# A hybrid decoder layer on one core: the recurrence's second pair mirrored in the array, attention's values channel-major, the first inverse ranked ahead

## The chip, the cores and the metric

The kernel is one launch on one NeuronCore of a Trainium2 chip. The metric is device time in microseconds (us). Before the change three runs took 1244.15, 1249.96 and 1253.78 us; the median is 1249.96 us.

## The reference, cut to what matters

One decoder layer on a sequence of 512 tokens of width 1024, all in fp32. A combined projection of the normalized input gives three attention groups, the inputs of an RWKV-7 recurrence and two branch gates; both mixers are projected, gated and added to the residual; a gated MLP with a short convolution follows.

```python
h = rms_norm(x, norm1_w) * (1 + sc1) + sh1             # sc1, sh1.. = c @ w_ada + b_ada
att_in, rwkv_in, gate_in = split(h @ w_in)
y_att  = attention_mixer(att_in) @ w_att_out            # 3 (window, dilation) groups of 8 heads x 64
y_rwkv = rwkv7_mixer(rwkv_in, ...) @ w_rwkv_out         # 16 heads x 64
x = x + gt1 * ((sig(g_att) * y_att + sig(g_rwkv) * y_rwkv) @ w_o)
x = rms_norm(x + gt2 * conv_ffn(adaLN(x)))
# recurrence, per head; state is 64 x 64
sa = state @ aa_t
state = state * w_t + sa (x) bb_t + v_t (x) k_t ;  y_t = state @ r_t
# attention: out = sum over groups of share_g * softmax(q k^T) v ; share_g from the groups' denominators
```

## The kernel before, in words

**Products.** A matmul with 512 columns is done three times on fp32r halves (high x high, low x high, high x low), so that the names `hhi`, `hlo`, `whi`, `wlo` recur. The halves of weights are made by ScalarE (`whi`) and VectorE (`wlo`, L1139). Small products are plain fp32; the trace has two records for each of them, so "x8" of a small product is four matmuls.

**Order.** From the start to the gates everything is written as tasks with an engine, a cost in us, a priority and a due rank (`Plan`, `pl.add`). A simulated run over these costs fixes one order for each engine, and each engine then takes its instructions in that order. The 512-column products of projections (`body`) have the lowest priority on TensorE and stand where the plan expected a gap; tasks of the recurrence (`C_` = 0) go first. VectorE's work for pair m of the recurrence has rank `V_ + 0.1 m` = 200 + 0.1 m, and the inverse of group g the rank `I_ + (0.1, 0.2, 0.5, 0.6)[g]`, `I_` = 200.15.

**Attention.** Groups 1 and 2 are held in one permuted order, so there are two sets of results, `o[0]` and `o[1]`. `attend` takes one token block `n` and one pair of heads `i` at a time: scores (tile `sc`), exponentials, transposes (`pt`, copied to `pts`), and `values` (tile `po`, L831 ff): for each head a matmul with 128 tokens of `pts` as weights and 64 channels of `v` as columns, which gives tokens on partitions. At the end VectorE scales `o` by each head's share (L1017), TensorE turns 32 blocks of 128 x 128 into channels (tile `pa`, L151) and adds the two groups on the way, and four DMAs store `att_d`. Tasks with `open` in their name, and with them the loads for the recurrence's pairs (L1256), come after all of this.

**Recurrence.** 16 heads are 8 pairs m of two heads; a group g is two pairs (i = 0, 1), so there are 4 groups. `pair` makes a pair's operands: `ar` (a and r of 64 tokens side by side), `bk`, its transpose `bkt`, the masked products `gt` (grams: tile `pg<-ar,bk` on TensorE, masked by VectorE at L1397). `inverse` solves a triangular system per chunk on VectorE (tiles `lt`, `tt`, L1453 to L1519) and ends with two sets of 32 x 32 products on TensorE (tile `pe`). `chain` then goes through 8 chunks c of 64 tokens, both pairs together:

- `state`: `xy` = `mbd` (the state) times `ar` for both pairs, 128 x 128 x 128, then four 64 x 64 x 64 products of `gt` and `uv` added to the half X of `xy`. R and X are the partition halves of results and of the unknowns; they swap from chunk to chunk and are the same for both pairs;
- ScalarE copies the half X (`xs`, L1621); `solve`: four products 64 x 64 x 64 into `u`; ScalarE copies them into `uv` (L1658);
- `update`: four products with 128 rows and 64 weight columns into `w` (trace: `u<-uv,bkt`), where the two heads of a pair go to the two partition halves by turns; VectorE makes the next `mbd` (L1641);
- `outs`: four products with 128 rows and 64 weight columns that are added to the half R of `xy` (trace: `xy<-uv,gt 128*64`), copied by ScalarE (L1652);
- every second chunk `values`: two products 128 x 128 x 128 (`u<-cen,v`).

Groups g and g + 2 share a room of SBUF, so the projections of group 2 start after chain 0, those of group 3 after chain 1. `t<-ident,yt` turns a chain's results at its end.

Of the kernel before, what the change touches and what calls it, by code (L numbers as in the profile page):

```python
# [128 lines left out]
class Layer:  # L129
# [502 lines left out]

    def mask2(self):
# [38 lines left out]
    def attention(self):  # L672
# [4 lines left out]
        o = [ap.tile([P, 4, ATT_W], F32, name="o0"), None]  # L677
# [110 lines left out]
        def attend(gi, hf, order, blocks, width, mask, V, ready, prio):  # L788
# [4 lines left out]
            for n, i, new, end in order:  # L793
# [37 lines left out]
                def values(n=n, i=i, d=d, new=new, end=end):  # L831
                    if new:
                        pos[n] = self.aps.tile([P, 256], F32, tag="po", name=self.n("po"), bufs=2)
                    vs = V(n)
                    for h in range(2):
                        cs = slice(i * P + h * 64, i * P + h * 64 + 64)
                        for j, v in enumerate(vs):
                            self.mm(pos[n][:, cs], d["pts"][:, h, j * P : (j + 1) * P], v[:, cs],
                                    new and h == 0 and j == 0, end and h == 1 and j == len(vs) - 1)

                def out(n=n, i=i, new=new):
                    c0, c1 = (i * P if new else 0), i * P + P
                    if gi and o[1] is None:
                        o[1] = ap.tile([P, 4, ATT_W], F32, tag="o1", name="o1")
                    nc.scalar.copy(o[gi][:, n, hf * 256 + c0 : hf * 256 + c1], pos[n][:, c0:c1])
# [11 lines left out]
                t = pe(0.9 * wd / 256, values, [t], S0, take=("po",) if new else (), give=("pts",), name="po")  # L857
# [110 lines left out]
        for _ in ada:  # L968
            pass

# [23 lines left out]
        scaled = []  # L994
        for gi in range(2):
# [19 lines left out]
            def scale(n, gi=gi, ea=ea):  # L1015
                ov = o[gi][:, n, :].rearrange("p (h e) -> p h e", h=8)
                nc.vector.tensor_tensor(ov, ov, ea[:, n, :].unsqueeze(2).to_broadcast([P, 8, 64]), op=ALU.mult)  # L1017
            t = dve(0.6, diff, [got[gi], *stats[gi]], name="al")
            t = sca(0.45, exps, [t], name="al")
            t = dve(1.2, share, [t], name="al")  # L1020
            scaled += [dve(0.7, lambda n=n, scale=scale: scale(n), [t, *outs[gi]], name="al") for n in range(4)]
        for i in range(4):
            d = {}

            def turn(i=i, d=d):
                d["pa"] = self.aps.tile([P, S], F32, tag="pt", name=self.n("pa"), bufs=2)
# [196 lines left out]
    def pair(self, g, i):  # L1223
# [98 lines left out]
        def a_row():  # L1322
# [3 lines left out]
            nc.vector.scalar_tensor_tensor(halves(d["ar"], 1), c8(d["k"]), ch(self.kkn), pex(), op0=ALU.mult,  # L1326
                                           op1=ALU.mult)
# [5 lines left out]
        ar = dve(0.75, a_row, [k, ex, gr["room"]])  # L1333
# [6 lines left out]
        def norm():  # L1340

            pn = d["pn"] = self.psx("pn")
# [3 lines left out]
        def norms():  # L1346
            if i == 0:
                gr["sq"] = gp.tile([P, 16], F32, tag="sq", name=self.n("sq"), bufs=1)
            for x in range(2):
                nc.scalar.copy(gr["sq"][64 - 64 * x : 128 - 64 * x, 8 * i : 8 * i + 8], d["pn"][64 * x : 64 * x + 64, :8])  # L1350
# [33 lines left out]
        def gram(q):  # L1384
# [4 lines left out]
            for cc in range(4):  # L1389
                col = (cc % 2) * 2 + cc // 2  # L1390
# [38 lines left out]
    def inverse(self, g):  # L1429
# [6 lines left out]
        I = I_ + (0.1, 0.2, 0.5, 0.6)[g]  # L1436
# [128 lines left out]
    def chain(self, g):  # L1565
# [18 lines left out]
        def values(c):  # L1584
            for i in range(2):
                self.mm(d["u"][:, i * P : (i + 1) * P], prs[i]["v"][:, c * C : (c + 2) * C], self.cen, i == 0, i == 1)

        def value(c, x):
            uv = uvs[c + x] = cw.tile([P, 256], F32, tag="uv", name=self.n("uv"), bufs=3)
            nc.scalar.copy(uv[64 * x : 64 * x + 64, :], d["u"][64 * x : 64 * x + 64, :])  # L1590
# [5 lines left out]
        norms, all_ = [], []  # L1596

        def vals(c):
            t = pe(0.54, lambda: values(c), [start, last_uv])
            for x in range(2):  # L1600
                uvd[c + x] = sca(0.38, lambda x=x: value(c, x), [t], C_ + 0.01 * x, take=("uv",))
        vals(0)
        for c in range(NCH):
            e, q, cp = c % 2, c // 4, (c % 4) // 2
            r0, x0 = (0, 64) if e == 0 else (64, 0)
            R, X = slice(r0, r0 + 64), slice(x0, x0 + 64)
            gt = lambda i, h, rows, cols, e=e, q=q, cp=cp: prs[i]["gt"][rows, e, 4 * q + 2 * cp + h, cols]
            s = {}

            def state(c=c, q=q, s=s, gt=gt, R=R, X=X):  # L1610
                xy = s["xy"] = ps("xy", bufs=2)
# [526 lines left out]
```

## Time and profile before

| what | us |
|---|---|
| runs, median of 3 | 1249.96 |
| the profiled execution, own time | 1247.44 |
| its span, first to last instruction | 1245.7 |
| TensorE busy in the span | 1197.4 |
| VectorE busy | 746.5 |
| ScalarE busy | 545.4 |
| GpSimd busy | 118.2 |

The profiled execution's own time is the span and 1.74 us around it, and lies 2.52 us below the median of the runs. In the profile PE is TensorE's matmuls, PEld its weight loads, DVE VectorE, ACT ScalarE, POOL GpSimd. A row of a timeline gives its start, its length and how many records it merges; matmuls overlap, so what one takes of the engine is the distance from its start to the next row's start, less an idle time that the next row shows in brackets.

### The profile page before, as it was taken

To read this page: it belongs to the slowest core of one execution; us is meant where nothing else is said; L and a number is where in the kernel's file an instruction comes from. 1 tells how busy PE (TensorE), PEld (TensorE's weight loads), DVE (VectorE), ACT (ScalarE), POOL (GpSimd) and SP (SyncE) were. 2 spreads that over 40 slices of the span, in tenths; PEclk is the share of its full clock that TensorE was granted. 3 is DMA by queue.
4 is the path that set the end of the run, shared out by engine and by line. 5 is a ranking of instruction groups with operands and counts; after the bars stand their busy time and mean duration, and the time that the engine had idled before them with its cause. 6 is when DMAs were issued, how large, how long until landed. Compare 5 with 4: busy or idle time off the path is not lost.

```text
span 1245.7 us, 18047 instructions
## 1 busy us (share of the span) xinstructions
PE 1197.4 (96%) x7012; PEld 976.5 (78%) x7012; DVE 746.5 (60%) x1242; ACT 545.4 (44%) x981; POOL 118.2 (9%) x235
## 2 busy tenths in 40 slices
PE   4999999999999999999999799999999999999997
PEld 3788878888787877777787577788888888878886
DVE  6697862422678968536896844555556566552235
ACT  4484522523566373455445343334443434442133
POOL 4000000000001013030002222214100000000001
PEclk9899999999999999999999789999999999999999
DMA  9745871130333332322330424571133332323331
GB/s 316 242 143 163 274 235 49 46 85 1 92 99 88 97 89 77 110 60 82 92 105 26 146 79 132 174 219 34 56 97 96 90 102 85 102 87 116 102 119 68
DMA packets 168900, 139.39 MB, mean 112 GB/s; under 512 B 8849, under 2 KB 150251, under 8 KB 168815
## 3 DMA queue, kind: packets, MB, share of 16 engines
q1 hardware_dynamic: 168671, 137.98, 36.5%
q8 instruction: 55, 0.90, 0.3%
q14 instruction: 30, 0.25, 0.1%
q10 hardware_dynamic: 144, 0.26, 0.1%
HBM read 127.65 MB, written 10.56 MB: 111 GB/s over the span
## 4 chain that ended last, share of the span: by engine, by line
PE 82%; DVE 8%; DMA 5%; ACT 2%; issue 1%; SPq 0%; POOL 0%; POOLq 0%; DVEq 0%; ACTq 0%
PE u L148 23%; PE o L148 13%; PE v L148 7%; PE pg L148 7%; PE qk L148 6%; PE xy L148 4%; PE pr L148 3%; DMA araw<-in_w_ada_dram 3%; PE k L148 3%; PE pa L148 2%; PE r L148 2%; PE early L148 2%; PE po L148 2%; PE sc L148 1%; PE pt L151 1%
## 5 line engine op out<-in xcount | busy, mean ns | idle before, releaser
L194 DVE TENSOR_TENSOR wlo<-raw,whi 128x1024 fp32r<-128x1024 f32 x67 | 84.1, 1255 | 151.0 <-ACT whi L193 150.9
L148 PE MATMUL u<-h2lo,whi 128*128 128x512 f32 (+2 forms) x368 | 142.3, 387 | 0.0
L148 PE MATMUL u<-h2hi,whi 128*128 128x512 f32 (+2 forms) x368 | 142.3, 387 | 0.0
L148 PE MATMUL u<-h2hi,wlo 128*128 128x512 f32 (+2 forms) x368 | 142.2, 386 | 0.0
L1136 ACT CAST whi<-raw 128x1024 fp32r<-128x1024 f32 (+2 forms) x73 | 72.5, 993 | 130.2 <-PE qk L148 49.5
L193 ACT CAST whi<-raw 128x1024 fp32r<-128x1024 f32 x67 | 70.3, 1049 | 112.0 <-PE o L148 53.8
L1139 DVE TENSOR_TENSOR wlo<-raw,whi 128x1024 fp32r<-128x1024 f32 (+2 forms) x73 | 84.2, 1154 | 22.9 <-ACT whi L1136 22.7
L148 PEld LDWEIGHTS u<-h2hi,wlo 128*128 128x128 f32 x368 | 68.9, 187 | 15.7
L148 PEld LDWEIGHTS u<-h2lo,whi 128*128 128x128 f32 x368 | 68.9, 187 | 15.7 <-POOL h2lo L405 0.2
L148 PEld LDWEIGHTS u<-h2hi,whi 128*128 128x128 f32 x368 | 68.9, 187 | 15.5
L1983 DVE SCALAR_TENSOR_TENSOR u<-u,cols,u 128x511 f32<-128x511 f32 x88 | 65.6, 746 | 4.2 <-ACT u L1981 2.7
L148 PE MATMUL qk<-hhi,wlo 128*128 128x512 f32 x160 | 63.9, 400 | 0.0
L148 PE MATMUL qk<-hlo,whi 128*128 128x512 f32 x160 | 63.6, 397 | 0.0
L148 PE MATMUL qk<-hhi,whi 128*128 128x512 f32 x160 | 63.5, 397 | 0.0
L148 PE MATMUL o<-whi,fhi 128*128 128x512 f32 x144 | 56.1, 390 | 0.3 <-DVE u L1983 0.3
L148 PE MATMUL o<-wlo,fhi 128*128 128x512 f32 x144 | 56.0, 389 | 0.0
L148 PE MATMUL o<-whi,flo 128*128 128x512 f32 x144 | 56.0, 389 | 0.0
L148 PE MATMUL pg<-hhi,wlo 128*128 128x512 f32 x128 | 52.0, 406 | 0.0
L148 PE MATMUL pg<-hlo,whi 128*128 128x512 f32 x128 | 51.8, 405 | 0.0
L148 PE MATMUL pg<-hhi,whi 128*128 128x512 f32 x128 | 51.3, 401 | 0.0
L810 DVE CUSTOM_DVE_ANT_0 sm<-sc,m 128x256 f32<-128x256 f32 (+1 forms) x64 | 24.0, 405 | 37.6 <-PE sc L148 36.5
L347 DVE SCALAR_TENSOR_TENSOR acc<-araw,cols,acc 128x1024 f32<-128x1024 f32 x28 | 35.9, 1282 | 17.2 <-DMA araw<-in_w_ada_dram 17.1
(404 smaller groups left out, 2824.0 us busy)
## 6 DMA issues: line engine op xcount, KB each, us to landing
raw<-in_w_in_dram SPq DMA_DIRECT2D x62, 512.0 KB
raw<-in_w_up_dram SPq DMA_DIRECT2D x44, 512.0 KB
araw<-in_w_ada_dram SPq DMA_DIRECT2D x32, 512.0 KB
raw<-in_w_down_dram SPq DMA_DIRECT2D x22, 512.0 KB
araw<-in_w_ada_dram SPq DMA_DIRECT2D x32, 256.0 KB
wvraw<-in_w_in_dram SPq DMA_DIRECT2D x20, 256.0 KB
gate_d<-gs SPq DMA_DIRECT2D x16, 256.0 KB
gate<-gate_d SPq DMA_DIRECT2D x16, 256.0 KB
```

Of the source, the lines that this page charges most:

```text
L148: return self.nc.tensor.matmul(out, lhsT, rhs, start=start, stop=stop)
L151: self.nc.tensor.matmul(out, in_, self.ident[: in_.shape[0], : in_.shape[0]], is_transpose=True, start=start, stop=stop,)
L193: self.nc.scalar.copy(hl[0], raw)
L194: (lo_eng or self.nc.vector).tensor_tensor(hl[1], raw, hl[0], op=ALU.subtract)
L347: nc.vector.scalar_tensor_tensor(d["acc"], raw, ck, d["acc"], op0=ALU.mult, op1=ALU.add)
L810: nc.vector.tensor_tensor_reduce(d["sm", h][:, :wd], d["sc"][h][:, :wd], m[:, 256 - wd : 256] if gi == 0 else m[:, :wd], 1.0, 3.0e38, op0= ...
L1136: nc.scalar.copy(d["w"][0], d["raw"])
L1139: nc.vector.tensor_tensor(d["w"][1], d["raw"], d["w"][0], op=ALU.subtract)
L1983: nc.vector.scalar_tensor_tensor(u[:, d:], pu[:, : S - d], ch(c), u[:, d:], op0=ALU.mult, op1=ALU.add)
```

## The change

Four things are done.

1. **The second pair is mirrored.** For pair i = 1 the halves R and X are swapped, in `ar`, `bk`, `gt` (index `x ^= i`), in the norms, and in the chain. `xy` now holds only the unknowns' half of both pairs (128 columns, pair 0 in one partition half, pair 1 in the other), a new tile `xo` holds the results' halves, and the state's product is done in two tasks, `state` and `state_out`, each with two matmuls of 64 weight columns. The four products of `state`, `solve` and `outs` are written with the pair as inner loop (`ih`), so that the pairs take turns.
2. **Copies follow.** `xs` and `out` copy 128 x 128 in place of 64 x 256; `uv` is two chunks in one tile, and the solved values are copied by two copies in a row in place of one. At the end of a chain two turns of `yts` by x are each followed by two half-size `y` operations.
3. **Attention's values** have 64 channels of `v` as weights and 128 tokens of `pts` as columns, with the two heads on the two partition halves by turns, so `o` is channel-major. The share of each head is turned (8 small transposes), split into a high and a low part, spread over the channels by 8 products with 40 rows and 512 columns (tile `pw`), multiplied by VectorE and added by GpSimd in place of ScalarE's copy. GpSimd writes the constant rows for this (`share_rows`).
4. **The inverse of group 0** has the rank `I_ - 0.2` = 199.95 (before 200.25), ahead of all pairs' ranks.

```diff
-        I = I_ + (0.1, 0.2, 0.5, 0.6)[g]
+        I = I_ + (-0.2, 0.2, 0.5, 0.6)[g]
...
-            r0, x0 = (0, 64) if e == 0 else (64, 0)
-            R, X = slice(r0, r0 + 64), slice(x0, x0 + 64)
+            R = [slice(64 * (e ^ i), 64 * (e ^ i) + 64) for i in range(2)]
+            X = R[::-1]
...
-                if c:
-                    for i in range(2):
-                        self.mm(xy[:, i * P : (i + 1) * P], prs[i]["ar"][:, c, :], mbd(i), i == 0, False)
-                for j, (i, h, cs) in enumerate(hs):
-                    self.mm(xy[X, cs], gt(i, h, R, X), s["uv"][R, cs], c == 0 and j == 0, j == 3)
+                for i in range(2 if c else 0):
+                    self.mm(xy[X[i], :P], prs[i]["ar"][:, c, X[i]], mbd(i), True, False)
+                for i, h, cs, ci in ih:
+                    self.mm(xy[X[i], cs], gt(i, h, R[i], X[i]), s["uv"][R[i], ci], c == 0 and h == 0, h == 1)
+
+            def state_out(c=c, s=s, R=R):
+                s["xo"] = ps("xo")
+                for i in range(2 if c else 0):
+                    self.mm(s["xo"][R[i], :P], prs[i]["ar"][:, c, R[i]], mbd(i), True, False)
...
-                for j, (i, h, cs) in enumerate(hs):
-                    self.mm(d["u"][X, cs], gt(i, h, X, X), s["xs"][X, cs], j == 0, j == 3)
+                for i, h, cs, _ in ih:
+                    self.mm(d["u"][X[i], cs], gt(i, h, X[i], X[i]), s["xs"][X[i], cs], h == 0, h == 1)
...
-            for i in range(2):
-                self.mm(d["u"][:, i * P : (i + 1) * P], prs[i]["v"][:, c * C : (c + 2) * C], self.cen, i == 0, i == 1)
+            for n, i, x in ((0, 0, 0), (0, 1, 0), (1, 1, 1), (1, 0, 1)):
+                r = 64 * (i ^ x)
+                self.mm(d["u"][r : r + 64, n * P : n * P + P], prs[i]["v"][:, (c + x) * C : (c + x + 1) * C], self.cen,
+                        n == 0, n == 1)
...
-            last_uv = sca(0.38, lambda s=s, X=X: nc.scalar.copy(s["uv"][X, :], d["u"][X, :]), [so])
+            last_uv = sca(0.28, lambda solved=solved: solved(0), [so])
+            last_uv = sca(0.28, lambda solved=solved: solved(1), [last_uv])
...
-                            self.mm(pos[n][:, cs], d["pts"][:, h, j * P : (j + 1) * P], v[:, cs],
-                                    new and h == 0 and j == 0, end and h == 1 and j == len(vs) - 1)
+                            self.mm(pos[n][h * 64 : h * 64 + 64, i * P : i * P + P], v[:, c0 : c0 + 64],
+                                    d["pts"][:, h, j * P : (j + 1) * P], new and j == 0, end and j == len(vs) - 1)
...
-                for n in range(4):
-                    self.tr(d["pa"][:, n * P : (n + 1) * P], o[0][:, n, i * P : (i + 1) * P], n == 0, False)
-                for n in range(4):
-                    self.tr(d["pa"][:, n::4], o[1][:, n, i * P : (i + 1) * P], False, n == 3)
+                self.mm(d["w", gi], self.heads[:, i * P : (i + 1) * P], self.share[gi], True, True)
...
+                nc.gpsimd.tensor_tensor(d["t"], o[0][:, i, :], o[1][:, i, :].rearrange("p (r j) -> p j r", r=4), op=ALU.add)
```

How the instructions stand: TensorE in chain 0, one chunk from `state` to after `solve`, before (sizes in the order are those of the result, so `64x64 x4` are four matmuls):

```order
L148 MATMUL xy_4403<-mbd_86,ar_3240 128x128
L148 MATMUL xy_4403<-mbd_87,ar_3358 128x128
L148 MATMUL xy_4403<-uv_4384,gt_3299 64x64 x4
L148 MATMUL pg_4210<-hlo,whi_4018 128x512
L148 MATMUL pg_4210<-hhi,wlo_4019 128x512
L148 MATMUL pg_4210<-hhi,whi_4018 128x512
L148 MATMUL pg_4210<-hlo,whi_4018 128x512
L148 MATMUL u_4082<-xs_4412,gt_3299 64x64 x4
L148 MATMUL pg_4210<-hhi,wlo_4019 128x512
```

The same place in the changed kernel:

```order
L148 MATMUL xy_4391<-mbd_86,ar_3232 64x128
L148 MATMUL xy_4391<-mbd_87,ar_3325 64x128
L148 MATMUL xy_4391<-uv_4376,gt_3357 64x64 x4
L148 MATMUL xo_4402<-mbd_86,ar_3232 64x128
L148 MATMUL xo_4402<-mbd_87,ar_3325 64x128
L148 MATMUL pw_4407<-lw,l2h_3777 128x512
L148 MATMUL pa_4408<-la,l2h_3777 128x512
L148 MATMUL pw_4407<-lw,l2l 128x512
L148 MATMUL pa_4408<-la,l2l 128x512
L148 MATMUL u_4066<-xs_4405,gt_3357 64x64 x4
L148 MATMUL pg_4122<-hhi,whi_4042 128x512
```

Two matmuls of the state are now four, of half the weight columns each, and stand on both sides of the 64 x 64 products; as many filler products stand between `state` and `solve`.

TensorE in chain 0 at the end of an even pair of chunks, `update`, `values` and `outs`, before:

```order
L148 MATMUL u_4082<-uv_4250,bkt_3241 64x64 x2
L148 MATMUL u_4082<-uv_4250,bkt_3359 64x64 x2
L148 MATMUL u_4082<-cen,v_3213 128x128
L148 MATMUL u_4082<-cen,v_3457 128x128
L148 MATMUL xy_4342<-uv_4250,gt_3299 64x64 x4
L148 MATMUL pg_4210<-hhi,wlo_4019 128x512
```

and now:

```order
L148 MATMUL u_4066<-uv_4222,bkt_3233 64x64 x2
L148 MATMUL u_4066<-uv_4222,bkt_3326 64x64 x2
L148 MATMUL u_4066<-cen,v_3196 64x128
L148 MATMUL u_4066<-cen,v_3399 64x128 x2
L148 MATMUL u_4066<-cen,v_3196 64x128
L148 MATMUL xo_4329<-uv_4222,gt_3357 64x64 x4
L148 MATMUL pg_4122<-hhi,wlo_4043 128x512
```

The three tasks stay together, and all of their products now have 64 weight columns.

VectorE at the start of group 0's inverse (`lt`, `tt`, `sup` are its tiles; `wlo`, `v`, `kk`, `rl` and the masked `gt` belong to later pairs), before:

```order
L1371 SCALAR_TENSOR_TENSOR kk_719_3636<-k_3604,cols,na_3423 128x512
L1471 TENSOR_TENSOR lt_3620<-lt_3620,rn_3578 128x1024
L1139 TENSOR_TENSOR wlo_3644<-raw_3543,whi_3643 128x1024
L1149 SCALAR_TENSOR_TENSOR v_3670<-v_3582,mu_122,sh 128x512
L1475 MEMSET lt_3620 128x32
L1478 COPY sup_3679<-lt_3620 128x14
L1479 MEMSET lt_3620 128x14
L1380 TENSOR_TENSOR rl_3673<-kk_719_3636,rh_3672 128x512
L1505 TENSOR_TENSOR tt_3656<-tt_3656,lt_3620 128x4
```

and now:

```order
L1411 SCALAR_TENSOR_TENSOR kk_723_3626<-k_3609,cols,na_3450 128x512
L1506 STREAM_TRANSPOSE lt_3635<-ld_3600 128x32x32
L1511 TENSOR_TENSOR lt_3635<-lt_3635,rn_3581 128x1024
L1182 SCALAR_TENSOR_TENSOR v_3673<-v_3585,mu_122,sh 128x512
L1515 MEMSET lt_3635 128x32
L1518 COPY sup_3680<-lt_3635 128x14
L1519 MEMSET lt_3635 128x14
L1172 TENSOR_TENSOR wlo_3660<-raw_3512,whi_3659 128x1024
L1437 TENSOR_TENSOR gt_3662<-pg_733_3663,mask 128x2x2x128
L1437 TENSOR_TENSOR gt_3662<-pg_734_3664,mask 128x2x2x128
L1545 TENSOR_TENSOR tt_3675<-tt_3675,lt_3635 128x4
```

From group 0's last mask to the end of its inverse VectorE has 87 instructions before and 82 now. On TensorE 1219 products of 512 columns stand ahead of group 0's first `pe` product before, and 1227 now, 8 of which are the new `pw` products of attention. Ahead of group 1's they are 1389 and 1435, of group 2's 1782 and 1784, of group 3's 1872 and 1880; ahead of the last grams of group 3 1815, with chain 2 in its third chunk, and now 1812, with chain 2 in its second.

## Rows read from the trace of the kernel before

**Rows 1.** The page, part 1: TensorE; and busy time of each engine by stretches (us from the start; PE, PEld, DVE, ACT, POOL busy, in brackets the instructions; then the granted clock, 1.00 being 2.4 GHz and 0.50 1.2 GHz, DMA share and GB/s). The cuts 434, 508 and 707 are the ends of the inverses of groups 0, 1 and 3, 645 is that of group 2, and 668 is the last mask of group 3.

```profile
PE 1197.4 (96%) x7012; PEld 976.5 (78%) x7012; DVE 746.5 (60%) x1242; ACT 545.4 (44%) x981; POOL 118.2 (9%) x235
...
345.00:434.00 89.00, 88.74 (x468) 71.23 (x466) 77.62 (x133) 49.56 (x78) 4.95 (x10) 1.00 0.34 94
434.00:508.00 74.00, 73.76 (x647) 58.11 (x646) 56.99 (x114) 39.08 (x81) 17.00 (x30) 1.00 0.32 94
508.00:645.00 137.00, 135.77 (x972) 106.79 (x972) 89.64 (x156) 67.67 (x125) 17.37 (x34) 1.00 0.29 82
...
668.00:707.00 39.00, 33.03 (x265) 25.38 (x264) 30.88 (x72) 15.92 (x36) 12.11 (x21) 0.89 0.35 113
707.00:773.00 66.00, 62.07 (x542) 48.09 (x543) 30.98 (x59) 30.41 (x68) 15.34 (x27) 0.86 0.27 80
```

**Rows 2.** The same view in steps of 5 us around the start of chain 3.

```profile
695.00:700.00 5.00, 2.73 (x30) 2.23 (x29) 4.79 (x10) 1.42 (x3) 2.64 (x3) 0.82 0.65 210
...
710.00:715.00 5.00, 3.00 (x69) 2.63 (x69) 3.13 (x6) 3.21 (x6) 0.00 (x0) 0.50 0.22 58
715.00:720.00 5.00, 4.15 (x24) 3.34 (x24) 4.92 (x9) 3.45 (x8) 0.00 (x0) 0.50 0.79 217
720.00:725.00 5.00, 5.00 (x25) 3.70 (x25) 3.02 (x7) 2.39 (x5) 1.27 (x2) 0.50 0.44 140
725.00:730.00 5.00, 5.00 (x33) 3.75 (x31) 1.89 (x5) 2.85 (x8) 0.00 (x0) 0.95 0.18 56
```

**Rows 3.** TensorE's timeline in chain 0 (start, length, operation, records merged).

```profile
464.69 0.40 PE L148 MATMUL pg<-hhi,whi 128*128 128x512 f32 x1
465.01 0.68 PE L148 MATMUL u<-xs,gt 64*64 64x64 f32 x8
465.62 0.50 PE L148 MATMUL pg<-hlo,whi 128*128 128x512 f32 x1
465.95 0.40 PE L148 MATMUL pg<-hhi,wlo 128*128 128x512 f32 x1
...
466.75 0.45 PE L148 MATMUL u<-uv,bkt 128*64 128x64 f32 x8
467.13 0.71 PE L148 MATMUL u<-cen,v 128*128 128x128 f32 x4
467.77 0.68 PE L148 MATMUL xy<-uv,gt 128*64 128x64 f32 x8
468.38 0.50 PE L148 MATMUL pg<-hhi,wlo 128*128 128x512 f32 x1
...
469.41 0.40 PE L148 MATMUL pg<-hhi,whi 128*128 128x512 f32 x1
469.65 0.61 PE L148 MATMUL xy<-mbd,ar 128*128 128x128 f32 x4
470.19 0.68 PE L148 MATMUL xy<-uv,gt 64*64 64x64 f32 x8
470.79 0.50 PE L148 MATMUL pg<-hlo,whi 128*128 128x512 f32 x1
...
473.65 0.45 PE L148 MATMUL u<-uv,bkt 128*64 128x64 f32 x8
473.94 0.63 PE L148 MATMUL xy<-uv,gt 128*64 128x64 f32 x8
474.50 0.50 PE L148 MATMUL pg<-hhi,whi 128*128 128x512 f32 x1
```

**Rows 4.** TensorE's timeline at the end of group 2's inverse.

```profile
645.73 1.20 PE L148 MATMUL pe<-lt,gt 32*32 32x32 f32 x64
646.86 0.50 PE L148 MATMUL pg<-hlo,whi 128*128 128x512 f32 x1
```

**Rows 5.** TensorE's timeline in attention: one `values`.

```profile
237.61 0.39 PE L148 MATMUL qk<-hhi,wlo 128*128 128x512 f32 x1
237.84 1.00 PE L148 MATMUL po<-v,pts 128*128 128x64 f32 x8
238.65 0.48 PE L148 MATMUL qk<-hhi,whi 128*128 128x512 f32 x1
```

**Rows 6.** The chain of waits: the first products after the last transfer of w_ada, and the end of attention (start, length, what).

```profile
188.34 2.20 PE v L148 x8
...
329.07 1.66 PE pa L151 x13
...
331.36 5.76 DMA att_d<-attT
...
337.19 0.60 ACT attT L1034
...
340.04 1.90 DMA l<-in_a_dram
```

**Rows 7.** VectorE's timeline: group 3's last mask and the last operation of its inverse; and TensorE's waits for VectorE's inverses (total us, times, longest).

```profile
666.99 0.68 DVE L1397 TENSOR_TENSOR gt<-pg,mask 128x512 f32<-128x512 f32 x1
...
706.42 0.71 DVE L1519 STREAM_TRANSPOSE lt<-tt 128x512 f32<-128x512 f32 x1
...
PE pe L148 <- DVE lt L1519: 3.2, 2, 2.9
```

**Rows 8.** Groups of GpSimd's instructions: its additions of two 128 x 512 tiles (busy us, mean ns of one, idle before them).

```profile
L1875 POOL TENSOR_TENSOR gate<-gate,gate 128x512 f32<-128x512 f32 x8 | 11.2, 1403 | 45.0 <-DVE gate L1874 45.0
```

More of the change, by code (lines that the diff above doesn't have):

```diff
@@ L631, in masks, with share_rows @@
                 pattern=[[-1, P]], channel_multiplier=1)
+    def share_rows(self):
+        nc = self.nc
+        self.heads = self.awl.tile([P, 2, S], F32R, tag="qk12", name="heads", bufs=1)[:40, 0, :]
+        t = self.awl.tile([P, 2, S], F32R, tag="qk02", name="share", bufs=1)[:40]
+        self.share = [t[:, gi, :] for gi in range(2)]
+        one = lambda r, c: self.ident[r, c : c + 8].unsqueeze(2).to_broadcast([r.stop - r.start, 8, 64])
+        h = self.heads.rearrange("p (h e) -> p h e", e=64)
+        for r, c in ((slice(0, 32), 0), (slice(32, 40), 32)):
+            nc.gpsimd.tensor_copy(h[r], one(r, c))
+        for x in self.share:
+            nc.gpsimd.tensor_copy(x[:32].rearrange("p (h e) -> p h e", e=64), one(slice(0, 32), 64))
     def mask2(self):
@@ L1013, in share @@
                 nc.vector.tensor_tensor(ea, ea, dn, op=ALU.mult)
[L1015 to L1017 removed]
             t = dve(0.6, diff, [got[gi], *stats[gi]], name="al")
             t = sca(0.45, exps, [t], name="al")
[L1020 to L1021 removed]
+            shares.append((dve(1.2, share, [t], name="al"), ea))
@@ new lines, in attention, with turn, hi, lo @@
+        parts = []
+        for gi in range(2):
+            d = {}
+            def turn(gi=gi, d=d):
+                d["ps"] = self.aps.tile([P, S], F32, tag="pt", name=self.n("pe"), bufs=2)
+                for n in range(4):
+                    self.tr(d["ps"][:8, n * P : (n + 1) * P], shares[gi][1][:, n, :], n == 0, n == 3)
+            def hi(gi=gi, d=d):
+                nc.scalar.copy(self.share[gi][:8], d["ps"][:8])
+            def lo(gi=gi, d=d):
+                nc.vector.tensor_tensor(self.share[gi][32:40], d["ps"][:8], self.share[gi][:8], op=ALU.subtract)
+            t = pe(0.48, turn, [shares[gi][0], heads], take=("pt",), name="pa")
+            t = sca(0.6, hi, [t], name="pa")
+            parts.append(dve(0.7, lo, [t], give=("pt",), name="pa"))
@@ new lines, in out @@
+            def out(i=i, d=d):
+                d["t"] = self.awl.tile([P, S], F32, tag="attT", name=self.n("attT"), bufs=2)
+                nc.gpsimd.tensor_tensor(d["t"], o[0][:, i, :], o[1][:, i, :].rearrange("p (r j) -> p j r", r=4), op=ALU.add)
+            ts = []
+            for gi in range(2):
+                t = pe(0.24, lambda gi=gi, turn=turn: turn(gi), [parts[gi]], take=("pt",), name="pa")
+                ts.append(dve(0.7, lambda gi=gi, scale=scale: scale(gi), [t, *outs[gi]], give=("pt",), name="pa"))
@@ L1037, in attention @@
+            t = pl.add("POOL", 1.2, out, ts, E_, take=("attT",), name="pa")
             pl.add("DMA", 0.8, lambda i=i, d=d: nc.sync.dma_start(self.att_d[:, i, :], d["t"]), [t], W_, lag=2.0,
@@ L1595, in chain @@
         mb, uvd, last_uv = [], {}, start
-        norms, all_ = [], []
+        norms, all_, used = [], [], []
         def vals(c):
             t = pe(0.54, lambda: values(c), [start, last_uv])
-            for x in range(2):
-                uvd[c + x] = sca(0.38, lambda x=x: value(c, x), [t], C_ + 0.01 * x, take=("uv",))
+            t = sca(0.38, lambda: value(c, 0), [t], C_, take=("uv",))
+            uvd[c] = uvd[c + 1] = sca(0.38, lambda: value(c, 1), [t], C_)
         vals(0)
@@ L1665, in chain @@
                 vals(c + 1)
-            ou = pe(0.47, outs, [last_uv], C_ + 0.02, name="xr")
-            yt = sca(0.38, out, [ou], C_ + 0.05, take=("yts",) if c == 0 else (), give=("xy",))
-            pl.join([ou] + ([up] if c < NCH - 1 else []), give=("uv",))
+            ou = pe(0.35, outs, [last_uv, so_], C_ + 0.02, name="xr")
+            yt = sca(0.29, out, [ou], C_ + 0.05, take=("yts",) if c == 0 else (), give=("xo",))
+            used.extend([ou] + ([up] if c < NCH - 1 else []))
+            if e:
+                pl.join(used, give=("uv",))
+                used = []
             d["yt", c] = yt
@@ L1675, in chain @@
         g2, gg, ys = {}, {}, {}
-        fin = []
+        fin, after = [], []
         for i in range(2):
```

125 lines of the change are left out of this document (72 added, 53 removed).

## The prediction

> **What bounds the kernel now.** I read the page's shares first: TensorE is busy for 96% of the span [rows 1]. A share is a mean, so I went on to busy time by stretches, cut where VectorE's inverses end. From 345 to 645 us TensorE has 298.3 of 300 us: time that is taken from its products there shortens the run one for one, so long as VectorE (77.6 of 89 us in the tightest of these stretches) delivers in time. From 668 to 707 it is otherwise. Group 3's last mask starts at 666.99, the last operation of its inverse at 706.42 [rows 7], and chain 3 can't start before that. Some 40 us of VectorE work in a row stand there, TensorE has 33.0 of 39 us and loses 3.9 more up to 773, and its granted clock falls to 0.50, that is from 2.4 to 1.2 GHz [rows 1, 2]. So there are two regimes: chains 0 and 1, in which TensorE's own time counts, and chain 2's second half, in which VectorE's inverse 3 counts and a shorter chain 2 only makes TensorE wait longer.
>
> **Prices on TensorE, from chain 0's timeline.** I use the distance from one start to the next. A 512-column product takes 0.24 us among its like (469.41 to 469.65), 0.32 to 0.33 just before or after small 64-wide tiles: each change of tile shape costs about 0.1. `solve`, four products of one pair of halves, takes 0.61 us (465.01 to 465.62). `update`, whose four products take the two result halves by turns, takes 0.29 (473.65 to 473.94); `outs`, as many products of the same 128 x 64 tiles into one half alone, takes 0.56 (473.94 to 474.50) [rows 3]. Ahead of a 128-wide task `update` takes 0.38 (466.75 to 467.13), so some 0.05 to 0.1 of the 0.56 is the change of shape, and four products cost about 0.50 in one half and 0.29 by turns. The trace has no solve with turns; `solve` and `state` change row halves as well as column halves. The nearest row is `pe`, 64 records of 32 x 32 tiles over all quarters in 1.13 us, 0.018 each [rows 4], where `solve` needs 0.076 each, so quarters on different rows and columns do overlap.
>
> **The change on the chain, per chunk.**
> - `solve`: 0.61 and about 0.10 each in the products ahead and behind, 0.81 before; by turns its four products fall by the same 0.21 to 0.22, to 0.59. −0.22.
> - `outs`: the same step, −0.22.
> - `state`: `mbd` 0.54, `gt` 0.60 [rows 3] and 0.10 for the change before the next product, 1.24. After: four products of half the weight columns, by turns, 0.27 each side of `gt` (half of 0.54 for each two), `gt` 0.60 − 0.22 = 0.38, and three shape changes (0.30): 1.22. −0.02. The split gives back in shape changes what it saves in turns.
> - `values`, every second chunk: 0.64 between two 128 x 64 tasks [rows 3]. Afterwards all three tasks have 64 weight columns, so two shape changes (0.20) go, and four half products by turns cost some 0.05 less. −0.25, −0.12 per chunk.
>
> Together −0.58 per chunk, −4.6 us per chain of 8; I take −4.5. The bounds: 0, if what turns by row halves doesn't overlap and only `outs` and `values` gain while `state` pays its changes; −7, if `state` too gains in full. The two copies of `uv` (0.28 planned each, for one of 0.38) lie beside the filler products that stand between the tasks; where there is none, a chunk waits 0.2 us more, 1.6 per chain.
>
> The Trainium skill, "TensorEngine Tiling (Array Packing)", section on tiling modes, says that a change of tiling mode drains the engine. The trace agrees: 0.32 against 0.24 for the same product [rows 3]. By that rule the split of the state's product is a loss and not a gain; the sum above already has it at the measured 0.1.
>
> **Attention.** Before 188 us TensorE's chain hangs on transfers of w_ada [rows 6], so that only groups after that count, some 30 with eight products each. One `values` takes 0.81 and 0.09 in the product behind it [rows 5]. Four products by turns, each with 128 columns: from `update`'s 0.29 per eight records of 64 columns I get about 0.5 to 0.6 for 128 columns, and two shape changes of 0.1 where there was one small one: −0.05 to −0.15 each. I take −2 (bounds 0 and −5). The combination: 32 turns at 1.66/13 = 0.128 [rows 6], 4.1 us, go; 8 small turns (at most 1.0) and 8 products of 512 columns at 0.33 (2.6) come: about nothing. But GpSimd's addition, 1.40 in its nearest rows [rows 8], takes the place of a 0.60 copy, and the chain from `pa` over two stores and copies to the load of `a` has it twice [rows 6]: +1.6 if that chain is the one that counts, 0 if filler hides it. I take +1.5.
>
> **Inverses.** The order has nearly the same number of 512-column products ahead of group 0's `pe` (1227 for 1219, eight of them the share products), so the new rank moves VectorE's work but hardly frees TensorE: 0. Ahead of group 1's `pe` there are 46 more, of which each is work that has to be done anyway; what is at risk is that VectorE, now behind, keeps them apart: +2 (bounds 0 and +5). Before, TensorE waited for inverses 3.2 us in all, 2.9 of it at group 3 [rows 7].
>
> Ahead of group 3's last grams there are 3 products and one chunk of chain 2 less, together with what chains 0 and 1 save. One chunk with its filler (eight products by 0.24, and 0.59 + 0.82 + 1.22 of the chain) is about 4.5; I take −4. Behind it the 40 us stay in a row, and VectorE's segment has one more chunk of chain 2 in it (two `mbd` and their like, about 0.3 each, and small turns): +2. Chain 2's own 4.5 are hidden behind it: 0. Chain 3 has idle time ahead and little beside it but its own length: −4.5.
>
> **Sum.** 1247.44 (the profiled execution) − 9 (chains 0, 1) − 2 + 1.5 (attention) + 2 (inverse 1) − 4 + 2 (inverse 3) + 0 (chain 2) − 4.5 (chain 3) = 1233.4. The median of the runs lies 2.5 us above the profiled execution; I split that, 1235.
>
> **Rivals.**
> - *Full gain.* Chain 2's time also counts, because its chunks free VectorE (the `mbd` and copies come earlier) and inverse 3 starts and ends earlier; the turns are worth the naive half of all small products. −4.5 more for chain 2, −2 per chain more in three chains (state in full), −2.5 for the waits of inverse 1 that stay out: 1247.4 − 14 − 13 ≈ 1221, with the offset 1222. For it: 0.018 us per record in `pe`, far below what I used. Against: shape changes.
> - *VectorE takes it back.* Chains 0 and 1 are shorter by 9, but VectorE, at 77.6 of 89 us [rows 1], sets when groups 1 and 2 start, so that the 9 become waits at `pe`: 1235 + 9 = 1244. Against: the waits of before, 0.3 at all inverses but group 3's [rows 7], leave some slack.
> - *No overlap of row halves.* `solve` and `gt` of `state` stay at 0.61 and 0.60, and `state`'s split adds 0.2. Per chunk −0.34 + 0.2 + 0.02 remain: about −1 per chain, −3 in all with attention −2 and the rest of the sum about zero: 1244. Against it stands `pe` [rows 4].
>   The Trainium skill, "TensorEngine Tiling (Array Packing)", section on restrictions and gotchas, says that tiles on different rows must not use one PSUM bank at the same time. In this kernel pairs write to one tile of results from both row halves; `pe` does it too, and takes 0.018 per record, which no serial 32 x 32 product could, so the trace bears the rule out little.
> - *Slower: the clock.* A shorter chain with as long a VectorE inverse leaves TensorE without filler ahead of chains 1 and 2, as at 695 to 725: there 5.97 + 3.93 = 9.9 us idle [rows 1], and after 712 about 2 + 4.15 + 5.00 us of products at half clock, of which half, 5.6, is lost [rows 2]. One such stretch costs 15.5 and cancels the gain; it decides from two on: 1235 + 31 = 1266, less what the forecast already had for inverse 1, 1264. Against: TensorE has 298 of 300 us busy there now.
>
> **How the numbers follow.** Chances: forecast .45, full gain .24, VectorE takes it back .16, no overlap .09, clock .06. About 1% is what measurement can tell from no change here, so faster means below 1237.5 and slower above 1262.5. The forecast's own spread (±6) lies below 1237.5 with some seven tenths: faster .32 + .24 ≈ .55; within .13 + .16 + .09 ≈ .39; slower .06. For the range I take the forecast with both ends of the unknown terms, the full gain down to 1216 and the two cases at 1244 with 7 above: 1216 to 1251.
>
> **What would show it.** In the profile after: `solve` of four products starting 0.4 instead of 0.6 before the next; `outs` likewise; state's split paying two more changes; in chain 0 and 1's stretches (434 to 645) some 9 us less; the 40 us between the last mask and the end of inverse 3 unchanged or longer, with the idle time of TensorE still there; chain 3 shorter by 4.5. Wrong would be: `solve` still at 0.6 (no overlap); new waits at `pe` of groups 1 and 2 with the clock at 0.50 outside 695 to 725 (the clock); a stretch from last mask to `pe` below 36 us (full gain).

## The result and the profile after

The changed kernel takes 1232.96 us (median of 4 runs, 1232.7 to 1233.84), the kernel before, beside it, 1249.1: the ratio is 0.9873, 95% interval 0.9848 to 0.9898. Forecast were 1235 and a range of 1216 to 1251. The profiled execution has a span of 1230.6 us, 15.1 less than before.

TensorE's line of the page and busy time by stretches of the changed kernel (columns as in [rows 1]); the cuts at 431, 513.5, 638.3 and 699.7 are the first `pe` products of the four groups, 490, 570 and 759.2 the turns at the ends of chains 0, 1 and 3, 655.7 the end of group 3's last mask.

```profile
PE 1177.4 (96%) x7172; PEld 926.6 (75%) x7172; DVE 751.1 (61%) x1256; ACT 541.3 (44%) x1007; POOL 122.0 (10%) x243
...
431.00:490.00 59.00, 58.34 (x636) 41.29 (x637) 39.11 (x86) 35.57 (x84) 14.76 (x31) 1.00 0.31 88
490.00:513.50 23.50, 21.02 (x94) 16.21 (x92) 22.81 (x37) 6.48 (x10) 0.00 (x0) 1.00 0.45 137
513.50:570.00 56.50, 56.30 (x627) 40.27 (x628) 28.24 (x53) 31.00 (x77) 12.79 (x26) 1.00 0.24 67
570.00:638.30 68.30, 65.88 (x347) 52.33 (x345) 58.95 (x104) 32.20 (x50) 2.53 (x7) 1.00 0.32 89
638.30:655.70 17.40, 17.40 (x265) 13.30 (x265) 13.60 (x24) 11.31 (x26) 1.54 (x4) 1.00 0.26 75
655.70:699.70 44.00, 35.40 (x345) 23.21 (x345) 34.81 (x85) 21.02 (x52) 14.62 (x25) 0.91 0.34 109
699.70:759.20 59.50, 55.28 (x580) 38.43 (x581) 28.57 (x54) 25.89 (x68) 13.25 (x24) 0.90 0.32 95
759.20:1230.60 471.40, 460.30 (x2046) 374.71 (x2043) 247.66 (x317) 178.28 (x258) 32.66 (x57) 1.00 0.34 105
```

TensorE's busy time fell by 20.0 us and its idle time grew by 4.9; the two make the 15.1. By stage, with the first `pe` of a group and the first turn of a chain read in both traces:

| stage | before | after | difference | forecast |
|---|---|---|---|---|
| start to group 0's `pe` | 434.3 | 431.1 | −3.2 | −0.5 |
| chain 0, `pe` to turns | 63.8 | 59.0 | −4.8 | −4.5 |
| chain 1 | 60.6 | 56.4 | −4.2 | −4.5 |
| turns of chain 0 to `pe` of group 1, and of chain 1 to group 2 | 87.0 | 91.8 | +4.8 | +2 |
| group 2's `pe` to the end of group 3's last mask | 21.9 | 17.4 | −4.6 | −4 |
| that to group 3's `pe` | 39.5 | 44.0 | +4.5 | +2 |
| chain 3 | 63.95 | 59.55 | −4.4 | −4.5 |
| its turns to the end | 474.6 | 471.4 | −3.2 | 0 |

The chain stretches came out as forecast to within 0.3 us each. The rest did not, and its errors cancel. The stretches do not hold the same filler, though: in the traces 129, 118 and 100 products of 512 columns stand in chains 0, 1 and 3 before, and 122, 113 and 114 now. At 0.23 us each that is −1.6, −1.2 and +3.3 us, so the lengths alone are no price of the mirrored pair.

TensorE's timeline in chain 0 of the changed kernel, which answers to [rows 3]:

```profile
457.25 0.44 PE L148 MATMUL xy<-mbd,ar 128*64 128x128 f32 x4
457.62 0.45 PE L148 MATMUL xy<-uv,gt 64*64 64x64 f32 x8
458.00 0.44 PE L148 MATMUL xo<-mbd,ar 128*64 128x128 f32 x4
458.37 0.50 PE L148 MATMUL pg<-hlo,whi 128*128 128x512 f32 x1
458.70 0.40 PE L148 MATMUL pb<-rh,bones 128*128 128x512 f32 x1
...
459.27 0.45 PE L148 MATMUL u<-xs,gt 64*64 64x64 f32 x8
459.64 0.50 PE L148 MATMUL pg<-hhi,wlo 128*128 128x512 f32 x1
...
461.62 0.45 PE L148 MATMUL u<-uv,bkt 128*64 128x64 f32 x8
461.90 0.61 PE L148 MATMUL u<-cen,v 128*64 128x128 f32 x8
462.34 0.40 PE L148 MATMUL xo<-uv,gt 128*64 128x64 f32 x8
462.67 0.50 PE L148 MATMUL pg<-hhi,wlo 128*128 128x512 f32 x1
```

From start to start: `solve` 0.37 (before 0.61), `outs` 0.33 (0.56), `values` 0.44 (0.64), `gt` of `state` 0.38 (0.60). `mbd` takes 0.37 on each side of it, 0.74 in place of 0.54, and all of `state` with the change behind it (458.37 to 458.70 is 0.10 longer than a product among its like) 1.12 + 0.10, as much as the forecast's 1.22 and hardly less than before.

The end of inverse 3 in the changed kernel, VectorE's rows and TensorE's (in brackets the wait and its releaser); they answer to [rows 7]:

```profile
663.07 0.61 DVE L1697 SCALAR_TENSOR_TENSOR mbd<-u,pc,mp 128x128 f32<-128x128 f32 x2 [2.87 <-PE u L148]
669.20 0.61 DVE L1697 SCALAR_TENSOR_TENSOR mbd<-u,pc,mp 128x128 f32<-128x128 f32 x2 [1.35 <-PE u L148]
...
697.36 0.69 DVE L1559 STREAM_TRANSPOSE lt<-tt 128x512 f32<-128x512 f32 x1
...
689.23 0.73 PE L148 MATMUL xo<-uv,gt 128*64 128x64 f32 x8 [0.36 <-ACT uv L1687]
695.48 0.47 PE L151 MATMUL t<-ident,yt 128*128 128x128 f32 x1 [5.05 <-POOL yt L1834]
697.58 1.09 PE L151 MATMUL t<-ident,yt 128*128 128x128 f32 x4 [1.62 <-DVE y L1798]
699.73 1.92 PE L148 MATMUL pe<-lt,gt 32*32 32x32 f32 x64 [1.06 <-DVE y L1798]
```

VectorE's longest wait for TensorE behind the last mask in the kernel before:

```profile
672.10 0.61 DVE L1641 SCALAR_TENSOR_TENSOR mbd<-u,pc,mp 128x128 f32<-128x128 f32 x2 [2.74 <-PE u L148]
```

The inverse is done at 698.05, but chain 2's turns, which stood behind group 3's `pe` before, now stand ahead of it on TensorE and wait for GpSimd and VectorE: 1.7 us between the inverse and `pe`, where before there was 0.1.

### The profile page after: what moved, and what is told of

Its sections match the earlier page's. It is cut to its first block, busy times and chain, and to the rows that moved or that the text cites. A ratio compares the mean times of both kernels' runs of the same rounds, so it can differ in the third digit from the quotient of the medians.

```text
span 1230.6 us, 18413 instructions
## 1 busy us (share of the span) xinstructions
PE 1177.4 (96%) x7172; PEld 926.6 (75%) x7172; DVE 751.1 (61%) x1256; ACT 541.3 (44%) x1007; POOL 122.0 (10%) x243
## 5 line engine op out<-in xcount | busy, mean ns | idle before, releaser
L347 DVE SCALAR_TENSOR_TENSOR acc<-araw,cols,acc 128x1024 f32<-128x1024 f32 x28 | 35.9, 1281 | 13.4 <-DMA araw<-in_w_ada_dram 13.2
```

The lines of the kernel that those rows point to most:

```text
L347: nc.vector.scalar_tensor_tensor(d["acc"], raw, ck, d["acc"], op0=ALU.mult, op1=ALU.add)
```

## The experiments

**Parts of the change by themselves.** The mirrored pair alone is the changed kernel with the old rank and with all of attention as before:

```diff
-        I = I_ + (-0.2, 0.2, 0.5, 0.6)[g]
+        I = I_ + (0.1, 0.2, 0.5, 0.6)[g]
...
-                    for j, v in enumerate(vs):
-                        for h in range(2):
+                    for h in range(2):
+                        cs = slice(i * P + h * 64, i * P + h * 64 + 64)
+                        for j, v in enumerate(vs):
...
```

> The mirrored second pair and its copies alone, attention's values and the rank of the first inverse as before. Theory (the chains carry the gain, chain 2's share hidden): chains 0, 1 and 3 each 4.4 to 4.8 us shorter, 10 to 14 us less than before in all. Rival (much of the gain comes from attention or from the new rank, since in the changed kernel group 0's first pe product stands 3.2 us earlier and the chain stage alone is only part of the 15): 5 to 9 us less.

Measured 1231.72 us, ratio 0.9866 (0.9852 to 0.988), 16.3 below before. All of the gain is the mirror's; the theory's 10 to 14 fell short by 2 us and the rival is out. The chain stretches of this kernel are 1.3, 3.0 and 3.7 us shorter, not 4.4 to 4.8 each: chain 0 holds 13 products of filler more than before.

Attention alone (before, with the new `values`, `share_rows`, `turn`, `scale`, `out`):

```diff
-                            self.mm(pos[n][:, cs], d["pts"][:, h, j * P : (j + 1) * P], v[:, cs],
+                            self.mm(pos[n][h * 64 : h * 64 + 64, i * P : i * P + P], v[:, c0 : c0 + 64],
...
```

> Channel-major attention values alone. Prediction's terms: -2 for values and +1.5 for the combination, so 0 to -1 us. Rival (values save 0.22 us in each of some 16 groups behind 190 us, against 0.05 to 0.15 forecast): group 0's first pe product 3 us earlier and 2 to 4 us less in all.

Measured 1250.45, ratio 1.0013 (0.9999 to 1.0027): no gain, perhaps a loss of up to 3 us. The rival is out, though TensorE's prices moved as it had them; of the theory's 0 to −1 only the end at 0 lies in the interval. One `values` and one share product in the changed kernel's timeline:

```profile
216.41 0.66 PE L148 MATMUL po<-pts,v 128*64 128x128 f32 x8
217.00 0.50 PE L148 MATMUL qk<-hhi,whi 128*128 128x512 f32 x1
...
329.68 0.49 PE L148 MATMUL pw<-share,heads 40*128 40x512 f32 x1
330.10 0.50 PE L148 MATMUL k<-hhi,wlo 128*128 128x512 f32 x1
...
334.50 0.50 PE L148 MATMUL r<-hhi,whi 128*128 128x512 f32 x1 [1.26 <-DVE lt L1182]
```

`values` takes 0.59 in place of 0.81 [rows 5], but the new `pw` takes 0.42 and not the 0.33 estimated, and TensorE waits 1.26 us for `lt`, which stands on VectorE behind the combination's new multiplications; the kernels with the old attention have no such wait there.

The rank alone, and the changed kernel without it:

```diff
-        I = I_ + (0.1, 0.2, 0.5, 0.6)[g]
+        I = I_ + (-0.2, 0.2, 0.5, 0.6)[g]
```

> The rank of group 0's inverse alone. Theory (TensorE has filler there, 1219 products ahead of the first pe either way): within 1 us of before. Rival (the inverse ends earlier and chain 0 starts earlier): 3 us less or more. Second rival (group 1's inverse is pushed back, as in the changed kernel, where it ends 5.5 us later): 2 to 5 us more.

Measured 1261.86, ratio 1.0114 (1.0087 to 1.014): 13.8 us slower, more than any expectation. Busy times in this kernel, and TensorE's wait:

```profile
417.00:427.00 10.00, 0.54 (x3) 0.11 (x1) 9.62 (x15) 1.67 (x3) 0.00 (x0) 0.78 0.45 116
427.00:432.00 5.00, 3.46 (x122) 3.33 (x124) 3.90 (x6) 4.30 (x7) 0.00 (x0) 0.50 0.02 3
706.00:770.00 64.00, 58.77 (x520) 45.44 (x519) 24.93 (x49) 29.64 (x67) 14.91 (x26) 0.84 0.40 123
```

```profile
427.13 1.92 PE L148 MATMUL pe<-lt,gt 32*32 32x32 f32 x64 [9.59 <-DVE lt L1519]
```

Group 0's `pe` comes 7 us earlier than before, but TensorE has nothing to do for 9.6 us ahead of it, since the fixed order puts the filler behind: counted in the trace, 1148 products of 512 columns stand ahead of that `pe`, against 1219 before. The expectation's "1219 either way" doesn't hold with the rank alone, and the 71 that are missing, at 0.23 us each, are about 16 us: the 7 and the 9.6. The granted clock drops there. In chain 3 it is low too (0.84), but so it was before (0.86 from 707 to 773 [rows 1]).

> The changed kernel with the old rank of the first inverse, 200.25. Theory (the rank is worth nothing): 1233 within 1 us. Rival (the rank is what pushes group 1's inverse back by 5.5 us): 2 to 5 us below the changed kernel, 1228 to 1231, and group 1's first pe product at or before 508 us. Rival on the other side (the rank is what lets chain 0 start 3 us earlier): 1235 to 1237.

Measured 1240.84, ratio 0.9938 (0.9923 to 0.9952): 7.9 us more than the changed kernel, further than the rival on the other side. So the same edit costs 13.8 alone and saves 7.9 with the other two. The mirror with the rank but without attention:

> The mirrored second pair with the new rank of the first inverse, attention as before. If the parts were independent: 1231.7 + 13.8 = 1245.5. Theory (what a rank does is decided by which waits the fixed order then leaves, as in the rank alone, where TensorE waits 9.6 us for group 0's inverse and slows down in chain 3): the wait at group 0 comes back, since no share products or later attention stand ahead of it, 1240 to 1247. Rival (the rank pays off once the chains are shorter, as between the kernel with mirror and attention and the changed one, 8 us): 1224 to 1230.

Measured 1242.39, ratio 0.996 (0.9943 to 0.9977): 10.7 above the mirror alone, in the theory's range, and by the theory's mechanism: again 1148 products stand ahead of group 0's `pe`, and TensorE waits 9.6 us for it:

```profile
430.50 1.92 PE L148 MATMUL pe<-lt,gt 32*32 32x32 f32 x64 [9.62 <-DVE lt L1526]
```

In the changed kernel it is 1227 products (eight of them `pw`) and a wait of 0.5. Attention with the rank alone wasn't run, so it is not shown whether attention by itself brings the products back ahead of `pe`.

I split each profiled span in steps of 5 us of the busy times: busy times granted clock is work at full speed, the rest of busy is what the lower clock took, and what is not busy is idle. The profiled execution of mirror and rank was the slowest of its ten (1248.1 for a median of 1242.39); the others lie within 3 us of their medians.

| kernel | full-speed work | lost to the clock | idle | span |
|---|---|---|---|---|
| before | 1185.0 | 12.4 | 48.3 | 1245.7 |
| attention alone | 1183.6 | 16.9 | 46.4 | 1246.8 |
| rank alone | 1183.4 | 18.5 | 55.6 | 1257.5 |
| mirror alone | 1167.4 | 13.1 | 50.3 | 1230.8 |
| mirror and attention | 1168.6 | 14.7 | 56.4 | 1239.7 |
| mirror and rank | 1169.5 | 16.2 | 60.8 | 1246.4 |
| all three (changed kernel) | 1169.4 | 8.0 | 53.2 | 1230.6 |

Work falls by 15 to 18 us wherever the mirror is, and by under 2 without it. Everything else, up to 16 us, lies in the last two of the three columns: what the planned order leaves in waits, and the clock after them.

**Turns or halves.** In the changed kernel the pair becomes the outer loop of the four products; tasks and their order are the same on every engine.

```diff
-            ih = [(i, h, slice(h * 64, h * 64 + 64), slice(i * P + h * 64, i * P + h * 64 + 64)) for h in range(2) for i in range(2)]
+            ih = [(i, h, slice(h * 64, h * 64 + 64), slice(i * P + h * 64, i * P + h * 64 + 64)) for i in range(2) for h in range(2)]
```

> The changed kernel with the pair as outer loop in state, solve and outs: the same instructions in the same tasks and the same order of tasks, only the four small products of a task now go pair by pair and not by turns. Theory (the gain is the overlap of products in different halves that stand next to each other): solve back from about 0.38 to 0.55-0.61 us, gt and outs likewise, about 0.6 us per chunk, 4.9 per chain; 15 us more than the changed kernel if chain 2's share is hidden behind inverse 3, 20 if it is not. Rival (the mirrored halves alone do it, whatever the order of the four, or the gain is in the tile changes): within 3 us of the changed kernel.

Measured 1237.13, ratio 0.9909 (0.9878 to 0.9941), 4.2 above the changed kernel by the medians. The theory's 15 to 20 is out, and so, narrowly, is the rival's "within 3". TensorE's timeline there:

```profile
456.92 0.45 PE L148 MATMUL xo<-uv,gt 128*64 128x64 f32 x8
457.30 1.16 PE L148 MATMUL pg<-ar,bk 64*128 64x128 f32 x16
458.40 0.44 PE L148 MATMUL xy<-mbd,ar 128*64 128x128 f32 x4
458.76 0.46 PE L148 MATMUL xy<-uv,gt 64*64 64x64 f32 x8
459.15 0.44 PE L148 MATMUL xo<-mbd,ar 128*64 128x128 f32 x4
...
460.42 0.46 PE L148 MATMUL u<-xs,gt 64*64 64x64 f32 x8
460.81 0.50 PE L148 MATMUL pg<-hhi,wlo 128*128 128x512 f32 x1
```

`solve` takes 0.39 and `gt` 0.39, 0.01 to 0.02 more than by turns, `outs` 0.38 (0.04 to 0.05 more). What counts is that two of the four products lie in another quarter; that they alternate is worth a few hundredths a task. In the profiled spans the 4.6 us between the two kernels are 1.8 of full-speed work and 3.3 of clock, less 0.6 of idle time.

**One chain at a time.** The same loop order in chain 2 or chain 3 alone (`if g == 2: ih = ih[0::2] + ih[1::2]`):

> Turns taken away in chain 2 alone, the order of tasks unchanged. Theory of the prediction (chain 2 is hidden behind inverse 3, which is VectorE's): 0 to 1 us more than the changed kernel. Rival (VectorE's mbd steps for chain 2 stand in its queue inside inverse 3 and wait for chain 2's products, so chain 2's length is part of the inverse's): 3 to 5 us more.

> Turns taken away in chain 3 alone, the order of tasks unchanged. Theory: chain 3 is on TensorE's path with filler between its tasks, 4.5 to 5 us more. Rival (chain 3's tasks wait for ScalarE and VectorE, and TensorE's share is hidden): 0 to 2 us more.

Measured 1234.87 (ratio 0.9889, 0.9863 to 0.9915) and 1235.04 (0.989, 0.9864 to 0.9916). Both lie between their two expectations, 1.9 and 2.1 above the changed kernel. With turns worth so little the dose is too small: 0.2 us between the two says nothing on chain 2. A larger dose repeats each `solve` of chain 2 (and, in a second kernel with `g == 3`, of chain 3):

```diff
-                for i, h, cs, _ in ih:
+                for i, h, cs, _ in ih * (3 if g == 2 else 1):
                     self.mm(d["u"][X[i], cs], gt(i, h, X[i], X[i]), s["xs"][X[i], cs], h == 0, h == 1)
```

> The changed kernel, with the four products of each solve of chain 2 issued three times (the second and third time the same results again), the order of tasks unchanged. Eight chunks by two more solves of some 0.35 to 0.4 us are 5.6 to 6.4 us of TensorE. Theory of the prediction (chain 2 is hidden behind inverse 3): 0 to 1.5 us more than the changed kernel's 1233, and group 3's first pe product within 1.5 us of the place it has in the kernel with the same edit in chain 3. Rival (chain 2's length is part of the stretch, by VectorE's waits for its products and by filler that comes later): 4 to 6.5 us more.

> The same edit in chain 3 alone. Theory (chain 3 stands among filler on a full TensorE): 5.6 to 6.4 us more than the changed kernel, about 1239. Rival (hidden by waits): under 2 us more. The two kernels of this pair are compared with each other first: 4 to 6 us between them if chain 2 is hidden, under 1.5 us if it is not.

Measured 1236.62 (0.9903, 0.9878 to 0.9927) and 1238.1 (0.9906, 0.9881 to 0.9932). They are 3.7 and 5.1 us above the changed kernel. One tripled `solve` of the kernel with the edit in chain 3; then in the one with chain 2 group 2's `pe`, the end of inverse 3 and the first turn of chain 3; then the first and the last of these in the kernel with chain 3:

```profile
733.51 0.92 PE L148 MATMUL u<-xs,gt 64*64 64x64 f32 x24
734.35 0.51 PE L148 MATMUL pa<-ahi,wlo 128*128 128x512 f32 x1
```

```profile
637.65 1.20 PE L148 MATMUL pe<-lt,gt 32*32 32x32 f32 x64
699.44 0.69 DVE L1559 STREAM_TRANSPOSE lt<-tt 128x512 f32<-128x512 f32 x1
762.21 0.60 PE L151 MATMUL t<-ident,yt 128*128 128x128 f32 x4
```

```profile
640.34 1.20 PE L148 MATMUL pe<-lt,gt 32*32 32x32 f32 x64
764.88 0.60 PE L151 MATMUL t<-ident,yt 128*128 128x128 f32 x4
```

Twelve products take 0.84 to 0.85 in nearly every chunk, not three times 0.37, so the dose was 3.7 us (eight times 0.84 less 0.38) and not 6. Most of it is seen in chain 2: from group 2's `pe` to the end of inverse 3 it is 62.5 us there and 59.7 in the changed kernel, 2.8 more, and group 3's `pe` is later by as much. From group 2's `pe` to the first turn of chain 3 the two kernels take the same, 124.6 and 124.5 us, where the changed kernel takes 120.9: the dose costs 3.6 in either place. By the times the two differ by 1.5 us, within their intervals, where 3.7 was to be seen if chain 2 were hidden; in the profiles 2.7 us between them arise ahead of group 2's `pe`, where their instructions are the same. The forecast that chain 2 is hidden is refuted by the trace and not supported by the times.

**One change of shape less.** `gt` ahead of `mbd` in `state`, so that the two `mbd` tasks of one shape can stand side by side:

```diff
-                for i in range(2 if c else 0):
-                    self.mm(xy[X[i], :P], prs[i]["ar"][:, c, X[i]], mbd(i), True, False)
                 for i, h, cs, ci in ih:
-                    self.mm(xy[X[i], cs], gt(i, h, R[i], X[i]), s["uv"][R[i], ci], c == 0 and h == 0, h == 1)
+                    self.mm(xy[X[i], cs], gt(i, h, R[i], X[i]), s["uv"][R[i], ci], h == 0, c == 0 and h == 1)
+                for i in range(2 if c else 0):
+                    self.mm(xy[X[i], :P], prs[i]["ar"][:, c, X[i]], mbd(i), False, True)
```

> The changed kernel with the two parts of state exchanged: the four 64 x 64 products of gt first, then the two products of mbd, so that these stand next to the two of state_out, which have the same shape. All tasks and their order stay. Theory (each change of tile shape costs about 0.1 us): one change less in most of 28 chunks, 1.5 to 3 us below the changed kernel. Rival (the changes are hidden, or filler that stands between state and state_out leaves as many): within 1 us.

> The same exchange in the kernel that has only the mirrored pair, with attention and rank as before the change. Expected by the same theory 1.5 to 3 us below that kernel's 1231.7, so 1229 to 1230; by the rival 1231 to 1232.5.

Measured 1231.96 (0.9862, 0.9835 to 0.9888) on the changed kernel, 1.0 below it, at the edge of the rival's range, and 1229.97 (0.9844, 0.9815 to 0.9873) on the mirror alone, as the theory had it. The first kernel's timeline:

```profile
456.75 0.45 PE L148 MATMUL xy<-uv,gt 64*64 64x64 f32 x8
457.13 0.44 PE L148 MATMUL xy<-mbd,ar 128*64 128x128 f32 x4
457.40 0.39 PE L148 MATMUL xo<-mbd,ar 128*64 128x128 f32 x4
457.72 0.50 PE L148 MATMUL pg<-hlo,whi 128*128 128x512 f32 x1
```

`state` takes 0.97 in place of 1.12, one shape change (0.10) and a little. Full-speed work is 2.2 and 1.9 us less than in the kernels it was made from. Each by itself is within the intervals; that the two went down by 1.0 and 1.7 us makes it likely, not shown. The last is the fastest median of all kernels here.

## Why the prediction was right, and where it was not

- **The chains: nearly right in size, in part by luck, and half right in cause.** −4.8, −4.2 and −4.4 for the forecast −4.5, and each task within 0.05 of its forecast. But chains 0 and 1 also hold less filler (1.6 and 1.2 us), and in chain 3, with 3.3 us more of it, 2.9 of the 4.4 are time that the lower clock no longer takes (6.9 before, 4.0 now, split as in the table above). The mirror's price is better read from the full-speed work: 15 to 18 us in four chains, about 4 each. The cause was named as turns between halves. The runs show halves: four products in one quarter take 0.61, two in each of two quarters 0.37 to 0.39 in either order (`outs`, in one column half or two: 0.56 and 0.33 to 0.38). I had read `update`'s 0.29 as the price of taking turns because its order was by turns; nothing in that row separates the two.
- **No overlap of row halves: refuted.** `solve` writes one tile from both row halves in 0.37. The Trainium skill, "TensorEngine Tiling (Array Packing)", section on restrictions and gotchas, says that different row tiles can't access the same PSUM bank at one time. If that meant that the two row halves run one after the other, `solve` would have stayed at 0.61, and the trace doesn't agree.
- **Attention, −0.5: wrong in its parts.** Its values saved more than forecast (0.22 each), but there are 16 of them behind 185 us and not some 30, `pw` cost 0.42 for an estimated 0.33, and alone it gained nothing (+2.4 by the medians). Full-speed work fell by 1.4; the clock took 4.5 more.
- **The rank, 0: the step that failed most.** "Moves VectorE's work but hardly frees TensorE" counted products ahead of `pe` in the changed kernel, and there the count is right. It belongs to that order and not to the rank: with the rank alone 71 products fewer stand ahead, TensorE has a hole of 9.6 us there and the kernel is 13.8 us slower; with the other two the rank is what holds the sum at 1233, by 7.9 (in the table 3.2 of idle time and 6.7 of clock, less 0.8 of work; what in the order does it is not shown).
- **Inverse 1, +2, and inverse 3, +2: too small**, +4.8 and +4.5. Group 1's `lt` ends 5.5 us later than before, yet TensorE waits only 0.3 us for it. Of its 4.9 us idle in the two stretches of that row (0.9 before) 3.2 are two waits for ScalarE's `gs`, of the gates, which the forecast didn't have:

```profile
507.63 0.50 PE L148 MATMUL r<-hhi,whi 128*128 128x512 f32 x1 [1.50 <-ACT gs L1849]
600.86 0.50 PE L148 MATMUL v<-hhi,whi 128*128 128x512 f32 x1 [1.67 <-ACT gs L1849]
```

  At group 3 VectorE's busy time behind the mask grew by 2.2 us, about as forecast for one chunk more; 1.6 us are the turns of chain 2 that now stand ahead of `pe`, a queue that the forecast didn't follow.
- **Chain 2, hidden: refuted** by the tripled `solve`. VectorE takes its instructions in order, and chain 2's `mbd` stand inside the inverse and wait for TensorE (2.87 and 1.35 us in the rows above). That was the full-gain rival's mechanism, but not its gain: such waits stood there before too (2.74 us), VectorE idles 9.1 us from the last mask to the end of inverse 3 where it idled 8.5, that end came only 1.7 us sooner after group 2's `pe`, and the turns took this back. From group 2's `pe` to group 3's it is 61.4 us for 61.5 before.
- **The tail, 0: −3.2.** From chain 3's turns to the end TensorE has 13 records and 3.2 us of busy time less; so that part of the filler was done earlier, in stretches that got longer.
- **Slower by the clock: not here, but real.** The rival's slump did come with the rank alone, ahead of group 0's `pe` and in chain 0, where the rival had put it ahead of chains 1 and 2; with 7.3 us more idle time and 6.1 more lost to the clock that kernel is 13.8 us slower.

So −13.4 for three chains (luck included), −4.6 ahead of the last mask and −6.4 at the two ends stand against +9.3 at the inverses, where −13.5, −4, −0.5 and +4 were forecast: the errors of 6.5 and 5.3 us cancel.

## What to carry to other kernels

Split every span into work at full speed, time lost to the clock and idle time before reading a difference: here work follows the edit, the other two follow the planned order, and a rank that is good beside one edit can be bad beside another. So test the parts of a change one by one: here two of three parts can be left out at no loss. The length of a stretch is a price only when the filler in it is counted too. Small products gained here by lying in different quarters of the array, in either order. To learn what is hidden, repeat one task in two places and compare the stretches in the traces; the times alone were too coarse for 3.7 us.

## What was not expected of the hardware

- Four 64 x 64 products in two quarters take 0.37 to 0.39 us whether they alternate or not; eight more of them in the same task add 0.47 (twelve take 0.84 to 0.85), so by estimate 0.14 of a lone `solve`'s 0.37, what four at that rate leave over, is start and shape change.
- Two neighbouring `mbd` tasks of one shape take 0.27 and 0.32 where the same tasks on both sides of another shape take 0.37 each.
- GpSimd's 128 x 512 addition takes 1.5 us twice in attention's end (two in 3.06) and 2.1 in the mean a little later (two in 4.15, the longest 2.45 by the profile), for 1.40 in [rows 8].
